# Small TensorE products and turned blocks widened to the whole 128x128 array

## The chip, the cores and the metric

The kernel runs on one core of a Trainium2 chip. The metric is the device time of one execution in microseconds (us), median over the runs shown. One further execution was taken by the hardware profiler; all rows quoted in this document that carry a time inside the kernel come from it.

## The reference

One step of a decoder layer is computed for a prompt of 512 tokens and for 8 sample sequences of 8 tokens each (64 sample tokens), 576 tokens in all, which share the weights (width 1024, fp32).

- Norm: `x * rsqrt(mean(x*x) + eps)`, ahead of and behind each of three blocks.
- Block 1 runs two mixers on one input projection. The first is a state-space scan with 16 heads and 2 groups. The second is an mLSTM with 4 heads (key width 128, value width 256): per head, `s = (q k^T) * D` with a decay matrix `D = exp(b_t - b_s + i_s - m_t)`, `num = s v + exp(..) q C`, `den = sum(s) + exp(..) q n`, `h = num / max(|den|, exp(-m_t))`, and new states `C`, `n`, `m`. The prompt starts from zero states; each sample sequence starts from states that are inputs and returns new ones.
- The mixers' normed and gated outputs go through one output projection (2048 to 1024). Block 2 is cross attention to 256 memory tokens with 4 heads of 256, block 3 a SwiGLU of hidden width 2816.
- Outputs are the 576 tokens, the memory's keys and values, and all new states.

## The kernel before

Activations are kept with features on the 128 partitions and tokens on the columns: 512 prompt columns, then 64 sample columns. A large product is made of fp32 factors split into a high and a low part, three products per 128x128 weight tile (L215, L216, L218), with weights streamed from memory.

The Python text lists the work in program order. A planner then orders the instructions of each engine along a simulated timeline: an instruction takes its turn when its inputs, its PSUM bank and its SBUF room are free, earlier ones in the text first. On the chip each engine works through its list in that order. `tc.issue_after(m)` holds instructions behind `m` on its engine. The framework puts a wait between two instructions whenever they touch an overlapping region of one tile and at least one writes it, and between the last use of a tile and the first use of another tile in the same room.

The parts that the change touches:

- **Norm rows.** `rstd_rows` (L279) turns a column of 1/rms values for each chunk of tokens into a row repeated on 128 partitions: a TensorE transpose per chunk, with the column broadcast to 128 as the stationary operand. The chunk of 64 sample tokens uses 64 rows of the array. It comes at the first norm, at the two group norms (`gn_apply`), behind the output projection, ahead of the cross attention, and once more in the tail by `root_rows1` (L2425).
- **Gates' columns.** Rows of per-token gate values, one per head, stand in `r1` (100 partitions) and in `r2` (4 partitions: the running maximum `mrw`). The transposes L617, L618, L621 and L622 turn them into `CT`, 104 columns per 128 tokens; two small products (L625, L632) with selector matrices fetch the values at chunk and sample ends.
- **State-space samples.** L788 makes one 64x64 product per group from the sample columns of `bc`.
- **mLSTM.** `qk` is one tile of 8 rows by 576 columns on 128 partitions: rows 0 to 3 are the queries of the four heads, rows 4 to 7 the keys. The prompt heads run in a loop (L957 to L1005): scores, decay, values, a chain of four 128-token states, a head norm, and at the end transposes (L1004) whose results are copied by ScalarE **over the prompt columns 0 to 511 of row h and of row 4+h of `qk`** (L1005). Behind the loop in the text come the samples: decay matrix `ds_` (L1013 to L1021), scores `ps_ss` of the four heads from columns 512 to 575 (L1024), their product (L1025), then for each half of four sequences the products with the old states (L1042 opens the sum in PSUM, L1049 adds to it), the states' update in place (`km` L1052, products L1056, VectorE L1057), the stores L1059, the product `ps_mx` of the maxima (L1066), a head norm, and a copy into columns 512 to 575 of `qk` (L1075).
- **What follows.** Gate projections (z from `z_evac` on, L1083; then og) stand later in the text. `mixs_h` and `mixs_l` (cast L202 and difference L203 in `gn_apply`) hold the first mixer's output; they lie in room that held the samples' pool `ms` and the tile `vt4_` (prompt values, and the samples' `es`). `out1` (L1181) is the output projection's first half and reads them; every later stage of block 1 reads its results.

Of the kernel before, what the change touches and what calls it, by code (L numbers as in the profile page):

```python
# [11 lines left out]
F32 = mybir.dt.float32  # L12
# [7 lines left out]
P = 128  # L20
T = 576
TP = 512
TS = 64
# [30 lines left out]
_c32 = {}  # L54
# [5 lines left out]
NC32, NLONG = _n, _c32["sgn"][0]  # L60
# [55 lines left out]
def build(nc, tc, ctx, I, O):  # L116
    V, A, G, S, TE = nc.vector, nc.scalar, nc.gpsimd, nc.sync, nc.tensor
    mm = TE.matmul
# [23 lines left out]
    def BP(name="b"):  # L142
        return pb.tile([P, 512], F32, name=name, tag="b")
# [11 lines left out]
    def C32(k):  # L155
        a, b = _c32[k]
        return c32[:, a:b] if b <= NLONG else c32e[:, a - NLONG:b - NLONG]
# [9 lines left out]
    ident, ones = C32("ident"), C32("ones")  # L167
# [65 lines left out]
    pows, ssq_mm, rops, rows = [], [], [], []  # L233
# [45 lines left out]
    def rstd_rows(rc, chunks, out, alloc=None, copy=None):  # L279

        for c0 in range(0, len(chunks), 3):
            part = chunks[c0:c0 + 3]
            b = part[0][0]
            w = part[-1][0] + part[-1][1] - b
            ps = (alloc or BP)("ps_rb")
            for j, (t0, n) in enumerate(part):
                rows.append(TE.transpose(ps[:, t0 - b:t0 - b + n], rc[:n, c0 + j:c0 + j + 1].to_broadcast([n, P]),
                                         ident[:n, :n]))
            (copy or A.copy)(out[:, b:b + w], ps[:, :w])
        return ps  # L290
# [24 lines left out]
    c32e = ml.tile([P, NC32 - NLONG], F32, name="c32e")  # L315
# [215 lines left out]
    qk = SL(1, "qk")  # L531
# [17 lines left out]
    def row(name, n=68, dt=F32, tag=None):  # L549
        return gp_.tile([n, T], dt, name=name, tag=tag or name)  # L550
# [19 lines left out]
    r1 = row("r1", 100)  # L570
# [5 lines left out]
    l2, gpr = row("l2", tag="e1"), row("gpr", tag="rmask")  # L576
    G.tensor_copy(l2[r4, :], la[r4, :])
# [5 lines left out]
    V.tensor_tensor_scan(mrw[r4, :], l2[r4, :], i2[r4, :], 0.0, op0=ALU.add, op1=ALU.max)  # L583
    G.memset(mp[r4, 0:128], 0.0)
# [29 lines left out]
    with tc.issue_after(products[140].ins), tc.high_priority(offset=1000):  # L614
        psc = MP("ps_ct")
        for c in range(4):
            TE.transpose(psc[:, c * 104:c * 104 + 100], r1[:, c * P:(c + 1) * P], ident[0:100, 0:100])  # L617
            TE.transpose(psc[:, c * 104 + 100:c * 104 + 104], r2[:, c * P:(c + 1) * P], ident[0:4, 0:4])  # L618
        A.copy(CT[:, 0:4, :], psc[:, 0:416].rearrange("p (c k) -> p c k", c=4))
        psc = MP("ps_ct2")  # L620
        TE.transpose(psc[:TS, 0:100], r1[:, TP:T], ident[0:100, 0:100])  # L621
        TE.transpose(psc[:TS, 100:104], r2[:, TP:T], ident[0:4, 0:4])  # L622
# [9 lines left out]
        mm(pse[:TS, 0:104], C32("esamp")[:TS, :], CT[:TS, 4, :], start=True, stop=True)  # L632
# [143 lines left out]
    for g in range(2):  # L776
# [11 lines left out]
        mm(pcb[:TS, :TS], bc[:, g, TP:T], bc[:, 2 + g, TP:T], start=True, stop=True)  # L788
# [233 lines left out]
    pss = BP("ps_ss")  # L1022
    for h in range(4):
        mm(pss[:TS, h * TS:(h + 1) * TS], qk[:, 4 + h, TP:T], qk[:, h, TP:T], start=True, stop=True, skip_group_check=True)  # L1024
# [7 lines left out]
    for h in range(4):  # L1032
        TE.transpose(psk[:TS, h * P:(h + 1) * P], qk[:, 4 + h, TP:T], ident)
    kws = ms.tile([TS, 4, P], F32, name="kws")
    V.tensor_tensor(kws, psk[:TS, :].rearrange("p (h k) -> p h k", h=4),
                    wendm[:TS, 4, :].unsqueeze(2).to_broadcast([TS, 4, P]), op=ALU.mult)
    for hb in range(2):
# [24 lines left out]
        m4 = ms.tile([4, 4, 32], F32, name="m4t", tag="m4t", bufs=1)  # L1062
        V.tensor_tensor(m4, C32("m4")[:4, :].rearrange("p (h t) -> p h t", h=4),
                        mrow[:, r].unsqueeze(1).to_broadcast([4, 4, 32]), op=ALU.mult)
        psx = BP("ps_mx")
        mm(psx[:, 0:1], m4.rearrange("p h t -> p (h t)"), ones[:4, :], start=True, stop=True)  # L1066
# [1355 lines left out]
    def root_rows1():  # L2422
        tail["ps"] = ps = B0("ps_rb")
        for c, (t0, n) in enumerate(HCHUNKS[1]):
            TE.transpose(ps[:, t0 - 256:t0 - 256 + n], tail["pf1"][:n, c:c + 1].to_broadcast([n, P]), ident[:n, :n])  # L2425
# [216 lines left out]
```

## Time and profile before

| | us |
|---|---|
| median of 3 runs | 1073.94 (1070.35 to 1074.08) |
| profiled execution, its own time | 1071.59 |
| its span (first to last instruction) | 1069.8 |
| TensorE busy in the span | 1060.1 |
| VectorE busy | 775.2 |
| ScalarE busy | 616.5 |
| GpSimd busy | 236.9 |

The profile names engines PE (TensorE matmul), PEld (its weight load), DVE (VectorE), ACT (ScalarE), POOL (GpSimd) and SP (SyncE, which issues most transfers); a q behind the name is the engine's sequencer. A group's row gives line, engine, operation, what it writes and reads, shapes and count, then shortest, median and longest duration in ns with the first and the last start in us. A row of the timeline gives the start in us and the duration in us; a matmul's duration covers its way through the array and overlaps the next, so the time that one takes from the engine is the distance between starts. "64*128 64x64" of a matmul means a stationary operand of 64 rows and 128 columns, and a moving operand of 64 rows and 64 columns.

### The profile page before, as it was taken

The page shows a single profiled execution, that of the slowest core. Times are in us where ns is not written, and L with a number is a line of the kernel's source. Part 1 is how long each engine was busy: PE and PEld are TensorE (multiplying, and loading weights), DVE is VectorE, ACT ScalarE, POOL GpSimd, SP SyncE. Part 2 cuts the span into 40 slices and gives each one's busy share as a digit, 9 for nine tenths or more (in the row PEclk, how much of TensorE's full clock was granted, in tenths as well). Part 3 has the DMA queues.
Part 4 walks back from the last instruction along what each step waited for, and adds up shares of the span by engine and source line. Part 5 has one row for each costly group of instructions (what it writes and reads, how often), then busy time and mean ns, then how long its engine had stood idle before and what let it go on. Part 6 is the DMA issues. An engine that isn't in the chain of part 4 may idle for free.

```text
span 1069.8 us, 20670 instructions
## 1 busy us (share of the span) xinstructions
PE 1060.1 (99%) x8060; PEld 1006.9 (94%) x8060; DVE 775.2 (72%) x1554; ACT 616.5 (58%) x1115; POOL 236.9 (22%) x308
## 2 busy tenths in 40 slices
PE   9999999999999999999999999999999999999997
PEld 8999887778999999999999989999999999999997
DVE  6798675658887898779755556776467887787556
ACT  6778533446654557666555535545566566656654
POOL 0453643313123131010244201100011111111000
PEclk9999999999999999999999999999999999999999
DMA  6676544426654349784568775743476688578532
GB/s 209 164 172 133 160 128 171 155 69 189 192 155 139 98 128 245 289 285 139 174 208 290 269 245 177 263 119 100 128 178 141 157 191 176 117 190 187 145 120 89
DMA packets 59829, 184.10 MB, mean 172 GB/s; under 512 B 6700, under 2 KB 12204, under 8 KB 59220
## 3 DMA queue, kind: packets, MB, share of 16 engines
q1 hardware_dynamic: 43316, 139.79, 39.2%
q0 software_dynamic: 15840, 42.21, 20.8%
q8 instruction: 63, 1.03, 0.4%
q10 hardware_dynamic: 576, 0.79, 0.2%
q14 instruction: 34, 0.28, 0.1%
HBM read 162.11 MB, written 20.65 MB: 171 GB/s over the span
## 4 chain that ended last, share of the span: by engine, by line
PE 96%; DVE 2%; DMA 1%; issue 0%; ACT 0%; SPq 0%; POOL 0%; DVEq 0%; POOLq 0%
PE ps_in L218 7%; PE ps_in L215 7%; PE ps_in L216 6%; PE ps_v L882 5%; PE ps_g L2111 3%; PE ps_u L2111 3%; PE ps_g L2110 3%; PE ps_u L2112 3%; PE ps_g L2112 3%; PE ps_u L2110 3%; PE ps_dn L2110 2%; PE ps_dn L2112 2%; PE ps_dn L2111 2%; PE ps_dn L215 2%; PE ps_dn L218 2%; PE ps_o L218 2%
## 5 line engine op out<-in xcount | busy, mean ns | idle before, releaser
L215 PE MATMUL ps_in<-uh,whi 128*128 128x320 f32 (+1 forms) x544 | 162.5, 299 | 0.0
L218 PE MATMUL ps_in<-uh,wlo 128*128 128x320 f32 (+1 forms) x544 | 162.1, 299 | 0.0
L216 PE MATMUL ps_in<-ul,whi 128*128 128x320 f32 (+1 forms) x544 | 161.3, 297 | 0.0
L191 ACT CAST whi<-raw 128x1024 fp32r<-128x1024 f32 (+1 forms) x98 | 99.1, 1013 | 83.6 <-PE ps_in L216 15.9
L198 DVE TENSOR_TENSOR wlo<-raw,whi 128x512 fp32r<-128x512 f32 (+2 forms) x91 | 86.7, 953 | 54.1 <-ACT whi L191 53.0
L218 PEld LDWEIGHTS ps_in<-uh,wlo 128*128 128x128 f32 x544 | 102.1, 188 | 2.3 <-issue 1.3
L215 PEld LDWEIGHTS ps_in<-uh,whi 128*128 128x128 f32 x544 | 102.2, 188 | 1.8 <-issue 0.8
L216 PEld LDWEIGHTS ps_in<-ul,whi 128*128 128x128 f32 x544 | 102.4, 188 | 0.5
L196 POOL DMA_DIRECT2D wlo<-win x31 | 27.3, 881 | 79.8 <-ACT wlo L195 72.6
L2110 PE MATMUL ps_g<-b,whi 128*128 128x288 f32 x144 | 42.4, 295 | 0.0
L2111 PE MATMUL ps_g<-b,whi 128*128 128x288 f32 x144 | 42.3, 294 | 0.0
L2111 PE MATMUL ps_u<-b,whi 128*128 128x288 f32 x144 | 42.2, 294 | 0.0
L2110 PE MATMUL ps_u<-b,whi 128*128 128x288 f32 x144 | 42.2, 294 | 0.0
L2070 DVE TENSOR_TENSOR wlo<-sw,whi 128x1024 fp32r<-128x1024 f32 (+1 forms) x26 | 29.6, 1140 | 17.1 <-ACT whi L2069 11.8
L2083 ACT CAST whi<-rawx 128x1024 fp32r<-128x1024 f32 (+1 forms) x26 | 25.6, 986 | 26.1 <-PE ps_dn L2111 13.3
L2060 ACT CAST whi<-raw 128x1024 fp32r<-128x1024 f32 (+1 forms) x26 | 25.6, 984 | 23.0 <-PE ps_g L2111 11.8
L198 POOL TENSOR_TENSOR wlo<-raw,whi 128x512 fp32r<-128x512 f32 x17 | 29.9, 1764 | 38.1 <-ACT whi L191 38.0
L215 PE MATMUL ps_xo<-qh,whi 128*128 128x288 f32 x128 | 38.2, 301 | 0.0
L216 PE MATMUL ps_xo<-ql,whi 128*128 128x288 f32 x128 | 37.8, 297 | 0.0
L216 PE MATMUL ps_o<-mixm_l,whi 128*128 128x256 f32 (+1 forms) x128 | 37.5, 293 | 0.0
L215 PE MATMUL ps_xq<-u2h,whi 128*128 128x320 f32 (+1 forms) x128 | 37.5, 295 | 0.0
L215 PE MATMUL ps_o<-mixm_h,whi 128*128 128x256 f32 (+1 forms) x128 | 37.4, 293 | 0.0
(828 smaller groups left out, 3898.4 us busy)
## 6 DMA issues: line engine op xcount, KB each, us to landing
raw<-win SPq DMA_DIRECT2D x35, 512.0 KB, 3.9
raw<-wout SPq DMA_DIRECT2D x14, 512.0 KB, 5.9
raw<-wxq SPq DMA_DIRECT2D x13, 512.0 KB, 5.3
raw<-wgate SPq DMA_DIRECT2D x13, 512.0 KB, 4.5
raw<-wup SPq DMA_DIRECT2D x13, 512.0 KB, 5.2
wlo<-win POOLq DMA_DIRECT2D x24, 256.0 KB, 5.2
kva<-vc SPq DMA_DIRECT2D x11, 512.0 KB, 6.3
raw<-wv SPq DMA_DIRECT2D x10, 512.0 KB, 3.9
```

Source lines behind the costliest of these rows:

```text
L191: casts.append(A.copy(hi[:, :n], raw[:, :n]))
L196: accs.append(G.dma_start(lo[:, a:b], src[:, a:b], accum_op=ALU.add))
L198: e.tensor_tensor(lo[:, a:b], raw[:, a:b], hi[:, a:b].bitcast(F32), op=ALU.subtract)
L215: mm(ps, wh, ah, start=i == 0, stop=False)
L216: products.append(mm(ps, wh, al, start=False, stop=False))
L218: m = mm(ps, tiles[order[c]][1], xh(order[c], t0, n), start=False, stop=c == len(tiles) - 1)
L882: mm(ps, a, b, skip_group_check=True, **kw)
L2060: s.c1 = A.copy(s.h1[:, s.all], s.r1[:, s.all])
L2070: V.tensor_tensor(s.l2[:, s.all], sw[:, s.all], s.h2[:, s.all].bitcast(F32), op=ALU.subtract)
L2110: mm(ps, wh, b[0][k], start=start and k == 0, stop=False, skip_group_check=True)
L2111: mm(ps, wh, b[1][k], start=False, stop=False, skip_group_check=True)
L2112: m = mm(ps, wl, b[0][k], start=False, stop=k == nk - 1, skip_group_check=True)
```

## The change

Operands that used part of the array are widened.

- A norm row's last chunk is turned from all 128 rows of the column, with the whole identity; 128 columns are written where 64 are used.
- `r1` has 104 partitions. GpSimd issues a transfer that copies `mrw` into partitions 100 to 103, and one transpose takes the place of each pair. `r2` stays for its other readers. `CT`'s unused partitions 64 to 127 of the sample block are zeroed, and L632 takes 128 rows and 128 columns of its selector.
- L788 takes 128 columns of `bc` instead of 64 as its stationary operand.
- The samples' scores take 128 columns of `qk` from column 512 on. A row has 576 columns, so the view runs over columns 512 to 575 of row 4+h and columns 0 to 63 of row 5+h. Row 7 has no next row; its 64 columns are copied by GpSimd to a zeroed tile `k3`.
- The maxima's factor `m4` is one zeroed tile of 128 partitions, of which four are filled, for both halves.

```diff
             for j, (t0, n) in enumerate(part):
-                rows.append(TE.transpose(ps[:, t0 - b:t0 - b + n], rc[:n, c0 + j:c0 + j + 1].to_broadcast([n, P]),
-                                         ident[:n, :n]))
+                rows.append(TE.transpose(ps[:, t0 - b:t0 - b + P], rc[:, c0 + j:c0 + j + 1].to_broadcast([P, P]), ident))
...
-    r1 = row("r1", 100)
+    r1 = row("r1", 104)
...
+    G.memset(CT[TS:P, 4, :], 0.0)
...
     V.tensor_tensor_scan(mrw[r4, :], l2[r4, :], i2[r4, :], 0.0, op0=ALU.add, op1=ALU.max)
+    G.dma_start(r1[100:104, :], mrw[r4, :])
...
         for c in range(4):
-            TE.transpose(psc[:, c * 104:c * 104 + 100], r1[:, c * P:(c + 1) * P], ident[0:100, 0:100])
-            TE.transpose(psc[:, c * 104 + 100:c * 104 + 104], r2[:, c * P:(c + 1) * P], ident[0:4, 0:4])
+            TE.transpose(psc[:, c * 104:c * 104 + 104], r1[:, c * P:(c + 1) * P], ident[0:104, 0:104])
...
-        TE.transpose(psc[:TS, 0:100], r1[:, TP:T], ident[0:100, 0:100])
-        TE.transpose(psc[:TS, 100:104], r2[:, TP:T], ident[0:4, 0:4])
+        TE.transpose(psc[:TS, 0:104], r1[:, TP:T], ident[0:104, 0:104])
...
-        mm(pse[:TS, 0:104], C32("esamp")[:TS, :], CT[:TS, 4, :], start=True, stop=True)
+        e0 = _c32["esamp"][0] - NLONG
+        mm(pse[:, 0:104], c32e[:, e0:e0 + P], CT[:, 4, :], start=True, stop=True)
...
-        mm(pcb[:TS, :TS], bc[:, g, TP:T], bc[:, 2 + g, TP:T], start=True, stop=True)
+        mm(pcb[:, :TS], bc.rearrange("p g t -> p (g t)")[:, g * T + TP:g * T + TP + P], bc[:, 2 + g, TP:T], start=True, stop=True)
...
+    k3 = ms.tile([P, P], F32, name="k3s")
+    G.memset(k3[:, TS:P], 0.0)
+    G.tensor_copy(k3[:, 0:TS], qk[:, 7, TP:T])
     for h in range(4):
-        mm(pss[:TS, h * TS:(h + 1) * TS], qk[:, 4 + h, TP:T], qk[:, h, TP:T], start=True, stop=True, skip_group_check=True)
+        k0 = (4 + h) * T + TP
+        mm(pss[:, h * TS:(h + 1) * TS], k3 if h == 3 else qk.rearrange("p j t -> p (j t)")[:, k0:k0 + P], qk[:, h, TP:T],
+           start=True, stop=True, skip_group_check=True)
...
+    m4 = ms.tile([P, 4, 32], F32, name="m4t")
+    G.memset(m4, 0.0)
...
-        m4 = ms.tile([4, 4, 32], F32, name="m4t", tag="m4t", bufs=1)
-        V.tensor_tensor(m4, C32("m4")[:4, :].rearrange("p (h t) -> p h t", h=4),
+        V.tensor_tensor(m4[:4], C32("m4")[:4, :].rearrange("p (h t) -> p h t", h=4),
                         mrow[:, r].unsqueeze(1).to_broadcast([4, 4, 32]), op=ALU.mult)
         psx = BP("ps_mx")
-        mm(psx[:, 0:1], m4.rearrange("p h t -> p (h t)"), ones[:4, :], start=True, stop=True)
+        mm(psx[:, 0:1], m4.rearrange("p h t -> p (h t)"), ones, start=True, stop=True)
...
         for c, (t0, n) in enumerate(HCHUNKS[1]):
-            TE.transpose(ps[:, t0 - 256:t0 - 256 + n], tail["pf1"][:n, c:c + 1].to_broadcast([n, P]), ident[:n, :n])
+            TE.transpose(ps[:, t0 - 256:t0 - 256 + P], tail["pf1"][:, c:c + 1].to_broadcast([P, P]), ident)
```

## The prediction

> **What bounds the kernel now.** I read the page's shares and the chain of waits first, then TensorE's timeline around each product that the change widens, then the groups of the mLSTM's samples, heads and successors.
>
> The page, busy shares and the chain that ended last:
>
> ```profile
> PE 1060.1 (99%) x8060; PEld 1006.9 (94%) x8060; DVE 775.2 (72%) x1554; ACT 616.5 (58%) x1115; POOL 236.9 (22%) x308
> PE 96%; DVE 2%; DMA 1%; issue 0%; ACT 0%; SPq 0%; POOL 0%; DVEq 0%; POOLq 0%
> ```
>
> TensorE sets the end nearly everywhere: whatever it is spared is gained, and whatever leaves it without work is lost, because nothing later has slack to give back.
>
> **What narrow products cost.** TensorE's timeline at a lone narrow norm row (L287), a pair of maxima products (L1066) and the gates' blocks:
>
> ```profile
> 524.30 0.28 PE L218 MATMUL ps_xq<-u2h,wlo 128*128 128x256 f32 x1
> 524.41 0.28 PE L215 MATMUL ps_xq<-u2h,whi 128*128 128x256 f32 x1
> 524.62 0.27 PE L287 MATMUL ps_rb<-c,p_r 64*128 64x64 f32 x1
> 524.82 0.38 PE L216 MATMUL ps_xq<-u2l,whi 128*128 128x256 f32 x1
> 525.04 0.28 PE L218 MATMUL ps_xq<-u2h,wlo 128*128 128x256 f32 x1
> ...
> 302.62 0.31 PE L218 MATMUL ps_in<-uh,wlo 128*128 128x320 f32 x1
> 302.86 0.38 PE L1066 MATMUL ps_mx<-c,m4t 4*128 4x1 f32 x2
> 303.17 0.41 PE L215 MATMUL ps_in<-uh,whi 128*128 128x320 f32 x1
> 303.42 0.31 PE L216 MATMUL ps_in<-ul,whi 128*128 128x320 f32 x1
> ...
> 81.25 0.25 PE L617 MATMUL ps_ct<-c,r 100*128 100x100 f32 x1
> 81.43 0.22 PE L618 MATMUL ps_ct<-c,r 4*128 4x4 f32 x1
> ...
> 83.06 0.42 PE L218 MATMUL ps_in<-uh,wlo 128*128 128x320 f32 x1
> 83.32 0.31 PE L215 MATMUL ps_in<-uh,whi 128*128 128x320 f32 x1
> ```
>
> The reader is to look at distances between starts. 128x256 products follow one another at 0.11 us (524.30 to 524.41). Around the narrow row they are 0.21, 0.20 and 0.22: the engine loses time going in, in the product, and coming out.
>
> Prices of the same work on the whole array, from the chain (a transpose block) and two groups (one-column sums; the scores):
>
> ```profile
> 284.03 0.87 PE ps_ht L1004 x8
> ...
> L241 PE MATMUL ps_ss<-c,ssqx x10: 250/250/271, 25.9 to 26.9; 128*128 128x1 f32 x10
> ...
> L1024 PE MATMUL ps_ss<-qk x8: 221/222/270, 224.3 to 224.7; 128*64 128x64 f32 x8
> ```
>
> A full transpose takes 0.87/8 = 0.11 us; a full product with one column takes (26.9 - 25.9)/9 = 0.11 per pass, so its 128-column weight load sets it; a score pass with 64 columns takes (224.7 - 224.3)/7 = 0.06.
>
> **The sum of the savings.**
> - Norm rows: 0.21 + 0.20 + 0.22 - 2 x 0.11 = 0.41 now, 0.11 after, 0.30 saved. Six of them (first norm, two group norms, behind the output projection, ahead of the attention, tail): 1.8 us.
> - Maxima: from 302.62 to 303.42 is 0.80, of which two 128x320 products at 0.15 are 0.30; 0.50 now, two passes of 0.11 after, 0.28 saved, twice: 0.6.
> - Gates: 81.25 to 83.32 less one product of 0.15 is 1.92 for ten transposes. After it four full ones (0.44) and one that still writes 64 partitions (0.11 + 0.30 for going in and out): 0.85. Saved 1.1. The selector product L632: two passes and two switches, like the maxima, 0.3. L788, two groups, likewise 0.3 each at the most, 0.5 together.
> - Scores: entry and exit saved (0.3 or less), but eight passes go from 0.06 to 0.11, which costs 0.4. Between -0.2 and +0.2; I take 0, the two rows being close.
>
> Together 4.3 us; 3 if the exits turn out to be other waits, 5 at the most.
>
> **What is added, at no cost while it is covered.** The zeroing and the copy for `k3`, `m4` and `CT` go to GpSimd, 22% busy, long ahead of use. The transfer of `mrw` waits on GpSimd's queue for the scan; ScalarE's copy of `sx` is the last writer of `r1` today:
>
> ```profile
> 73.74 1.35 DVE L583 TENSOR_TENSOR_SCAN mrw<-l,i 4x576 f32<-4x576 f32 x1
> ...
> 75.21 0.86 POOL L196 DMA_DIRECT2D wlo<-win  x1 [5.21 <-DVE mrw L583]
> ...
> 80.27 0.67 ACT L595 COPY r<-sx 4x576 f32<-4x576 f32 x1
> ...
> wlo<-win POOLq DMA_DIRECT2D x24, 256.0 KB, 5.2
> ```
>
> The scan ends at 75.1; issue 0.9 and landing 5.2 (a far larger transfer, so an upper bound) give 81.2 at the latest, against 80.9 for `sx` and 81.25 for the first transpose. A weight transfer (75.21) is queued behind it and moves 0.9 back. While either is late, TensorE has input projection products to run, so I cost both at 0; without that cover, 0.3 and 0.9 us.
>
> **The new wait.** The view for head h reads columns 0 to 63 of row 5+h. ScalarE writes these at the end of prompt head h+1 (L1005), and that copy stands earlier in the text, so TensorE must now wait for it: score 0 for head 1, score 1 for head 2, score 2 for head 3, the last. L1025 needs all four. Groups of the heads and of the samples, then VectorE's and ScalarE's steps:
>
> ```profile
> L971 PE MATMUL ps_s<-qk x32: 270/275/276, 250.6 to 351.7; 128*128 128x128 f32 x32
> L1005 ACT COPY qk<-ps_ht x8: 571/589/595, 285.6 to 385.6; 128x512 f32<-128x512 f32 x8
> ...
> 317.52 1.07 ACT L1005 COPY qk<-ps_ht 128x512 f32<-128x512 f32 x2 [0.36 <-PE ps_ht L1004]
> 347.30 1.07 ACT L1005 COPY qk<-ps_ht 128x512 f32<-128x512 f32 x2 [1.24 <-PE ps_ht L1004]
> ...
> L1025 DVE TENSOR_TENSOR ds__3161<-ds__3161,ps_ss x1: 402/402/402, 259.6 to 259.6; 64x256 f32<-64x256 f32 x1
> L1061 DVE COPY nums<-ps_nh x2: 419/423/427, 267.2 to 315.1; 128x257 f32<-128x257 f32 x2
> L1052 ACT ACTIVATE km<-sta,c x8: 708/724/726, 261.9 to 338.9; 96x512 fp32r<-96x512 f32 x8
> L1057 DVE SCALAR_TENSOR_TENSOR c<-c,vt,ps_cu x32: 473/477/486, 265.8 to 345.4; 128x258 f32<-128x258 f32 x32
> ```
>
> Today the scores run at 224.3 and the samples run inside the heads' time: L1025 at 259.6, the last state update at 345.4, while the last head's copy starts at 385.6. After the change everything from L1025 on starts behind that copy. Queued behind it by data are the sums L1042 and L1049, the in-place updates L1057 (the old state must be read first), the stores, and then whoever wants the samples' room:
>
> ```profile
> 365.40 0.37 ACT L1075 COPY qk<-ps_hts 128x256 f32<-128x256 f32 x1
> ...
> L202 ACT CAST mixs_h<-xs x8: 667/674/680, 365.7 to 369.7; 128x576 fp32r<-128x576 f32 x8
> L203 DVE TENSOR_TENSOR mixs_l<-xs,mixs_h x8: 745/752/806, 367.0 to 373.8; 128x576 fp32r<-128x576 f32 x8
> L215 PE MATMUL ps_o<-mixs_h,whi x32: 276/304/367, 385.0 to 397.1; 128*128 128x256 f32 x16, 128*128 128x320 f32 x16
> ```
>
> The casts start 0.3 us after the samples' last copy; they are their successor in the same room. TensorE reaches their product at 385.0, so today 19.3 us lie between.
>
> Working out when that product can start:
> - Heads: the copies of heads 1 and 2 are 347.30 - 317.52 = 29.8 us apart. Four such steps from 250.6, plus the pair of copies 1.1, give 371. Without the samples' share of VectorE they may be shorter (32 updates x 0.48 = 15 us in about 100, so 25 each: 352); as now, 386.
> - Samples behind it: from L1025 to `nums` 267.2 - 259.6 = 7.6 among other work, I take 6; per sequence `km` 0.72, four updates 4 x 0.48 and 0.7 for handing over, 3.3, times eight 26.7; 5 between the halves, whose split operands (`stacks`) have one buffer; 2 at the end. Together 40. Bounds: 33 without any handing over; 60, half way to today's 106 (259.6 to 365.4) among all the other work.
> - Casts and differences 0.67 + 0.75, and then the product runs at the pace of eight differences, 6.0, instead of its own 8 x 3 x 0.11 = 2.7: 4.7.
>
> 371 + 40 + 4.7 = 415.7, against 385.0: **30.7 us late**. Gate projections stand ahead of this in TensorE's order and need no more time than today, so nothing is left to fill the gap; all later work moves along. Bounds: 352 + 33 + 4.7 gives 5 us, 386 + 60 + 4.7 gives 66 us. I take the middle one, since its head step is measured and its updates are too.
>
> [...] The last slice of the profile, where TensorE runs dry, has a lower granted clock, and everything around it has a full one:
>
> ```profile
> 1050.00:1060.00 10.00, 10.00 (x90) 10.00 (x89) 7.80 (x14) 5.67 (x13) 0.00 (x0) 1.00 0.34 122
> 1060.00:1070.00 10.00, 2.98 (x25) 2.50 (x23) 4.31 (x12) 1.40 (x4) 0.00 (x0) 0.83 0.28 105
> ```
>
> (Columns: busy PE, PEld, DVE, ACT, POOL; then the granted clock 1.00 and 0.83.) [...]
>
> Net 30.7 - 4.3 = +26.4. The profiled execution took 1071.6 (span 1069.8, 1.8 around it), so 1098.0; the runs' median is 1073.9, 2.3 above that execution, and I leave the forecast at **1098 us**.
>
> **Rivals.**
> - *The stall is hidden; only the savings count.* The samples' late start would have to fit ahead of 385.0, so the heads would have to end by about 340. For it: VectorE loses 15 us of competing work there. Against it: each head's chain of four states is serial, and no head took under 29.8. 1071.6 - 4.3 = 1067.3. Chance 0.10. This is the case on the other side, and it also holds if the planner sees no overlap of the regions.
> - *The samples stay as slow behind the heads as within them.* Output gating and the sums for the next stage still want VectorE, and the state transfers (a store, then a load into the same buffer) would pace each half. The decisive point is whether a sequence takes over 5 us instead of 3.3: eight times 2 and a slower start and end give 60 instead of 40, 1118; with the heads at 386, 1133. Chance 0.13.
> - *The gates' transfer lands late.* If a small transfer took over 6 us and the input products ran out, the mixers would start up to 3 us later: 1101 with the stall, 1070 without. Chance of the second 0.03.
> - *Widening saves nothing.* If the switches are paid elsewhere, since other narrow products stay: 1102 with the stall, 1072 without it; the second has 0.02.
>
> **Chances and range.** The main case has 0.72, with 1079 to 1120 as its own range. No change means within 0.5%, about 5.4 us, of the median 1073.9. 1067.3 is 6.6 below it but only 4.3 below the profiled execution, so the hidden case is split: 0.05 faster, 0.05 same. Same gets 0.05 more from the small cases and 0.03 from the main case's low end: 0.13; slower 0.82. The range leaves out the hidden case, part of the slow one and the extremes: 1072 to 1121.
>
> **What would show it.** The scores L1024 start after the last L1005 copy instead of at 224, in four steps behind heads 1 to 3. TensorE has idle time between the last gate projection and `ps_o<-mixs_h`, ended by the casts or by VectorE, 20 to 45 us. The head step falls below 31 us. Narrow rows at 0.11 between starts, with no wide gap around them, would confirm the savings; the gates' block at 0.9 instead of 1.9. The prediction is wrong if the scores still start near 224, if TensorE stays above 98% busy, or if the heads end near 340.

## The result, and the profile after

The changed kernel takes 1111.1 us (median of 4 runs, 1109.5 to 1113.0) against 1072.6 for the kernel before on the same chip (4 runs, one more than in the table ahead of the prediction): ratio 1.0368, 95% interval 1.0353 to 1.0383. That is 38.6 us more, and the span of the profiled execution grew by the same amount, from 1069.8 to 1108.4. The forecast was 1098: slower was right, and the time lies within the range, but the loss is half as large again as forecast. One execution among all those below (1150.6 us at a mean granted clock of 0.85, in the run with more cover) stands apart and has no part in the ratios.

In the changed file the lines behind the edits stand four to seven lower: the scores are L1028, their product with the decay L1030, the sums L1049 and L1056, `km` L1059, the state products L1063 and updates L1064, the maxima L1072, the samples' turned blocks and their copy L1080 and L1081. L1005 is still the heads' last copy.

The page of the changed kernel: busy shares, TensorE's row and its granted clock in 40 slices, the chain that ended last.

```profile
PE 1073.5 (97%) x8055; PEld 1013.5 (91%) x8055; DVE 782.6 (71%) x1554; ACT 618.7 (56%) x1115; POOL 239.8 (22%) x313
PE   9999999999999858999999999999999999999997
PEclk9999999999999958999999999999999999999999
PE 84%; DVE 8%; issue 3%; ACT 3%; POOL 1%; DMA 0%; SPq 0%; DVEq 0%; ACTq 0%; POOLq 0%
```

TensorE still issues the same work, but slices 14 to 16 (about 360 to 443 us) show holes, and the clock falls to half in slice 15 (388 to 416 us). VectorE's and ScalarE's share of the chain rises from 2% and 0% to 8% and 3%. So there is one place to look at. The windows around it (columns: busy PE, PEld, DVE, ACT, POOL; then granted clock, DMA share, GB/s):

```profile
380.00:400.00 20.00, 10.07 (x47) 5.21 (x47) 11.64 (x32) 6.79 (x11) 0.88 (x2) 0.59 0.58 182
400.00:420.00 20.00, 12.39 (x60) 6.04 (x60) 9.29 (x28) 3.42 (x8) 1.15 (x2) 0.59 0.45 167
```

The groups that answer to those of the prediction (shortest, median and longest ns, first and last start):

```profile
L1005 ACT COPY qk<-ps_ht x8: 581/590/606, 284.3 to 376.4; 128x512 f32<-128x512 f32 x8
...
L1028 PE MATMUL ps_ss<-qk x6: 222/275/323, 318.9 to 377.2; 128*128 128x64 f32 x6
L1030 DVE TENSOR_TENSOR ds__3158<-ds__3158,ps_ss x1: 403/403/403, 377.9 to 377.9; 64x256 f32<-64x256 f32 x1
L1064 DVE SCALAR_TENSOR_TENSOR c<-c,vt,ps_cu x32: 470/482/485, 380.1 to 415.3; 128x258 f32<-128x258 f32 x32
L202 ACT CAST mixs_h<-xs x8: 667/668/672, 420.2 to 424.2; 128x576 fp32r<-128x576 f32 x8
L215 PE MATMUL ps_o<-mixs_h,whi x32: 276/304/581, 420.9 to 434.8; 128*128 128x256 f32 x16, 128*128 128x320 f32 x16
```

The scores, at 224 us before, now run from 318.9 to 377.4. The whole chain of the samples starts at 377.9 instead of 259.6, the casts at 420.2 instead of 365.7, and the output projection at 420.9 instead of 385.0. TensorE's timeline shows who ends each wait (in brackets: idle time before, and the releaser):

```profile
377.03 0.43 PE L1028 MATMUL ps_ss<-qk 128*128 128x64 f32 x2 [1.05 <-ACT qk L1005]
...
378.39 0.64 PE L1049 MATMUL ps_nh<-vts,ds__3158 32*32 32x257 f32 x8 [0.70 <-DVE ds__3158 L1030]
...
399.29 0.69 PE L1080 MATMUL ps_hts<-c,hns 128*128 128x128 f32 x2 [5.38 <-DVE hns L1077]
399.91 1.08 PE L1049 MATMUL ps_nh<-vts,ds__3158 32*32 32x257 f32 x8
...
407.13 0.80 PE L1063 MATMUL ps_cu<-stb,km 96*128 96x258 f32 x2 [0.87 <-ACT km L1059]
...
410.13 0.80 PE L1063 MATMUL ps_cu<-stb,km 96*128 96x258 f32 x2 [0.87 <-ACT km L1059]
...
419.08 0.69 PE L1080 MATMUL ps_hts<-c,hns 128*128 128x128 f32 x2 [3.03 <-DVE hns L1077]
...
420.92 0.85 PE L215 MATMUL ps_o<-mixs_h,whi 128*128 128x256 f32 x2 [1.15 <-ACT mixs_h L202]
```

The last wait for the heads is the first row, as the prediction had it; then comes the samples' own serial work, and the last row is the cast. The 5.38 in the middle was not in the prediction in that size: in TensorE's list the second half's sums stand behind the turned blocks of the first half's head norm, and they started behind them (399.91 against 399.29).

### The profile page after: what moved, and what is told of

It is laid out like the page before. It is cut to its first block, busy times and chain, and to the rows that moved or that the text cites. A ratio compares the mean times of both kernels' runs of the same rounds, so it can differ in the third digit from the quotient of the medians.

```text
span 1108.4 us, 20669 instructions
## 1 busy us (share of the span) xinstructions
PE 1073.5 (97%) x8055; PEld 1013.5 (91%) x8055; DVE 782.6 (71%) x1554; ACT 618.7 (56%) x1115; POOL 239.8 (22%) x313
## 4 chain that ended last, share of the span: by engine, by line
PE 84%; DVE 8%; issue 3%; ACT 3%; POOL 1%; DMA 0%; SPq 0%; DVEq 0%; ACTq 0%; POOLq 0%
PE ps_v L882 4%; PE ps_in L215 4%; PE ps_in L218 4%; PE ps_in L216 4%; PE ps_g L2117 3%; PE ps_u L2117 3%; PE ps_g L2116 3%; PE ps_u L2118 3%; PE ps_g L2118 3%; PE ps_u L2116 3%; PE ps_dn L2116 2%; PE ps_dn L2118 2%; PE ps_dn L2117 2%; PE ps_dn L218 2%; PE ps_dn L215 2%
## 5 line engine op out<-in xcount | busy, mean ns | idle before, releaser
L215 PE MATMUL ps_in<-uh,whi 128*128 128x320 f32 (+1 forms) x544 | 161.2, 296 | 0.1
L198 DVE TENSOR_TENSOR wlo<-raw,whi 128x512 fp32r<-128x512 f32 (+2 forms) x91 | 87.6, 962 | 54.7 <-ACT whi L191 53.7
L215 PEld LDWEIGHTS ps_in<-uh,whi 128*128 128x128 f32 x544 | 102.2, 188 | 1.1 <-DVE tmp L1151 0.3
L2089 ACT CAST whi<-rawx 128x1024 fp32r<-128x1024 f32 (+1 forms) x26 | 25.6, 986 | 26.4 <-PE ps_dn L2117 13.3
L198 POOL TENSOR_TENSOR wlo<-raw,whi 128x512 fp32r<-128x512 f32 x17 | 30.0, 1765 | 38.5 <-ACT whi L191 38.4
L215 PE MATMUL ps_xo<-qh,whi 128*128 128x288 f32 x128 | 38.2, 301 | 0.0
L215 PE MATMUL ps_o<-mixm_h,whi 128*128 128x256 f32 (+1 forms) x128 | 37.5, 293 | 0.0
L215 PE MATMUL ps_xq<-u2h,whi 128*128 128x320 f32 (+1 forms) x128 | 37.4, 295 | 0.0
```

The costliest lines, as they stand in the source:

```text
L198: e.tensor_tensor(lo[:, a:b], raw[:, a:b], hi[:, a:b].bitcast(F32), op=ALU.subtract)
L215: mm(ps, wh, ah, start=i == 0, stop=False)
```

## The experiments

Every ratio below is to the kernel before, run on the same chip, with a 95% interval. Four questions were open: is it the wait alone; how does the loss grow with the lateness; does the half clock in the gap belong to the cost; and where did the forecast savings of 4.3 us go.

### Only the scores undone

```diff
-    k3 = ms.tile([P, P], F32, name="k3s")
...
     for h in range(4):
-        k0 = (4 + h) * T + TP
-        mm(pss[:, h * TS:(h + 1) * TS], k3 if h == 3 else qk.rearrange("p j t -> p (j t)")[:, k0:k0 + P], qk[:, h, TP:T],
+        mm(pss[:TS, h * TS:(h + 1) * TS], qk[:, 4 + h, TP:T], qk[:, h, TP:T],
```

> The changed kernel with the four sample scores put back to 64x64, each reading only its own head's 64 sample columns; everything else of the change stays. Theory (the whole loss comes from the wide view that reads the first 64 columns of the next row of qk, so scores wait for the heads): the samples go back inside the heads, the gap on TensorE near 377 to 421 us goes, and what is left are the savings of the other edits, forecast 4.3 us (3 to 5): about 1068 us, ratio to before 0.996. Rival A (the loss sits in another edit: the transfer of mrw, the norm rows, the gates' block): still above 1100. Rival B (the other edits save nothing that reaches the end): 1072 to 1073, ratio 1.000.

Measured: 1073.7 us, ratio 1.0023 (1.0012 to 1.0033). The scores run at 218.7 to 227.4 again and the gap is gone. So the loss was the scores, but the forecast of what is left was wrong: the other edits do not save 4 us, they cost 2. Neither theory nor rival B had that.

### The same width without the overlap

```diff
+    k4 = ms.tile([P, 4, TS], F32, name="k4s", tag="hns", bufs=1)
+    G.tensor_copy(k4, qk[:, 4:8, TP:T])
...
-        mm(..., k3 if h == 3 else qk.rearrange("p j t -> p (j t)")[:, k0:k0 + P], ...
+        mm(..., k3 if h == 3 else k4.rearrange("p h t -> p (h t)")[:, h * TS:h * TS + P], ...
```

> The changed kernel with scores still 128 columns wide, but from a copy that holds only sample keys: the four heads' 64 sample columns side by side (heads 0 to 2 read their own and the next head's sample columns, which no head writes in this copy), and the zero-padded tile for head 3 as in the change. Width, shape and number of products stay as changed; only the overlap with columns 0 to 63 of the next row is gone. Theory (the overlap costs, the width doesn't): within 1 us of the run with narrow scores, about 1068. Rival (the wide products themselves, or their place behind a GpSimd copy, make the delay): above 1100, as changed.

Measured: 1074.5 us, ratio 1.0030 (1.0018 to 1.0043); the interval overlaps that of the narrow scores. 128 columns neither cost nor save anything that can be measured; what costs is that the 128 columns were read where the heads write.

### The scores alone, and the moment alone

The kernel before with nothing but the wide scores:

> The kernel before with only the scores widened exactly as in the change (with its padded tile for head 3). Theory: it alone carries the loss, without the savings of the other edits: after's 1111.1 + 4.3 = about 1115 us (1111 to 1119), TensorE idle 35 to 45 us behind the heads. Rival (the loss needs another edit): 1072 to 1080.

And the kernel before with its 64x64 scores, only issued late:

```diff
     for h in range(4):
-        mm(pss[:TS, h * TS:(h + 1) * TS], qk[:, 4 + h, TP:T], qk[:, h, TP:T], ...
+        with tc.issue_after(ht.ins):
+            mm(pss[:TS, h * TS:(h + 1) * TS], qk[:, 4 + h, TP:T], qk[:, h, TP:T], ...
```

> The kernel before with the 64x64 scores as they are, but issued on TensorE only behind the last head's turned blocks. Nothing is widened; only the moment is that of the change. Theory (it is the moment alone): 1111 to 1117 us, with the same gap behind the heads, perhaps 1 us less as there is no wait for ScalarE's last copy. Rival (the wide reads cost in some other way, by width or by traffic): near 1074.

Measured: 1110.3 us, ratio 1.0365 (1.0351 to 1.0379), and 1110.7 us, ratio 1.0373 (1.0358 to 1.0387). The wide scores alone give the whole loss, and so do narrow ones at the same moment. The group rows of the late narrow scores, and of the output projection behind them:

```profile
L1025 PE MATMUL ps_ss<-qk x8: 222/222/270, 374.6 to 375.0; 128*64 128x64 f32 x8
...
L215 PE MATMUL ps_o<-mixs_h,whi x32: 276/306/580, 420.0 to 434.4; 128*128 128x256 f32 x16, 128*128 128x320 f32 x16
```

The product starts at 420.0, against 420.9 in the changed kernel. The first run is 5 us under the 1115 of its theory and just under its range, the second just under its own range: both theories took away savings of the other edits that, by the first experiment, are not there. With or without the other edits the ratio is the same.

### How late is too late

Heads not named in the edit read copies of sample keys (`k4`) as above; head 0 alone, or heads 0 and 1, read `qk` 128 columns wide.

```diff
+        mm(..., k3 if h == 3 else k4.rearrange("p h t -> p (h t)")[:, h * TS:h * TS + P] if h >= 1 else
+           qk.rearrange("p j t -> p (j t)")[:, k0:k0 + P], ...          # second run: h >= 2
```

> The changed kernel where only the score of head 0 reads qk 128 columns wide, so it waits for head 1's last copy alone (near 316 us); heads 1 to 3 read copies that hold only sample keys. Theory (the later the scores, the more of the samples' work stands behind the heads, and each part of it costs its length there): before, the samples took 105 us between 260 and 364 us inside the heads and 43 us behind them. From 316 to the heads' end near 378, 60% of it is done inside and 40% is left, 0.4 x 43 = 17 us behind; the first out1 product at about 396, against 387 with narrow scores: about 1073.7 + 9 = 1083 us (1078 to 1090). Rival (only a wait that outlasts the heads costs; anything earlier is hidden): 1073 to 1076. Rival (whatever starts behind head 0 is paced by the last transfer or by the order, not by the moment): above 1100.

> The same with the scores of heads 0 and 1 wide in qk, so that the scores wait for head 2's last copy (near 351 us). Theory: from 351 to 377 a quarter of the samples is done inside the heads, three quarters stand behind them, 0.75 x 43 = 32 us; about 1073.7 + 23 = 1097 us (1090 to 1104). Rival (only a wait that outlasts the heads costs): 1073 to 1078.

Measured: 1091.2 us, ratio 1.0173 (1.0155 to 1.0192), and 1104.0 us, ratio 1.0300 (1.0284 to 1.0316). The last scores and the first output product, of the first run and then of the second:

```profile
L1030 PE MATMUL ps_ss<-qk,k3s x2: 275/275/275, 321.2 to 321.3; 128*128 128x64 f32 x2
L215 PE MATMUL ps_o<-mixs_h,whi x32: 276/304/582, 402.3 to 416.4; 128*128 128x256 f32 x16, 128*128 128x320 f32 x16
```

```profile
L1030 PE MATMUL ps_ss<-qk,k3s x2: 275/275/275, 356.0 to 356.1; 128*128 128x64 f32 x2
L215 PE MATMUL ps_o<-mixs_h,whi x32: 276/304/582, 414.3 to 428.5; 128*128 128x256 f32 x16, 128*128 128x320 f32 x16
```

So a wait that ends well inside the heads costs as well, and the rival "only a wait that outlasts the heads" falls. Against narrow scores (ratio 1.0023, scores at 227) the loss in us of 1072 is 16 with scores at 321, 30 at 356 and 37 at 377: 0.39 us for each us of lateness between the first two, 0.34 between the last two. Drawn back to nothing, that line starts at about 280, so the first 53 us of lateness would be free. At 0.39 these are 21 us, near the 19.3 that lay between casts and output projection before; no run between 227 and 321 tests this. The slope is near 43/105 = 0.41, the samples' length behind the heads over their length inside. Both runs lie above the forecast (8 and 7 us). In the first, the estimate of what stands behind the heads was right (402.3 is 16 us behind the last head copy at 386.0, forecast 17), but I had let the heads end at 378 as in the changed kernel; with half the samples inside them they end at 386. The rest is the slower pace of the output projection, 3.7 us here too (402.3 to its second half at 447.3, against 385.0 to 426.3 before), which I had left out.

### The clock in the gap

```diff
     cu = mm(ps[:, 0:258], km[:, h * P:(h + 1) * P], vst[:, h * 258:(h + 1) * 258], start=True, stop=True)
+    with tc.issue_after(cu.ins):
+        for _ in range(3):
+            mm(fill[:, 0:256], uh[:, 0, 0:P], uh[:, 0, 0:256], start=True, stop=True, skip_group_check=True)
...
+    with tc.issue_after(mx.ins):                    # behind the product of the maxima
+        for _ in range(24):
+            mm(fill[:, 0:256], uh[:, 0, 0:P], uh[:, 0, 0:256], start=True, stop=True, skip_group_check=True)
```

> The changed kernel with products that nothing reads put into TensorE's waits behind the heads: three full 128x128 fp32r products of 256 columns behind each of the 32 state products, 24 behind each product of the maxima. Theory (the clock that the gap leaves, 0.59, lengthens the samples' chain): the granted clock from 380 to 420 us goes above 0.8, the gap shortens by 3 to 7 us, 1104 to 1108 us. Rival (the chain runs on VectorE and ScalarE, TensorE's clock is not on it): within 1 us of 1111, or a few us above where the added products stand in the way.

Measured: 1109.4 us, ratio 1.0336 (1.0309 to 1.0363); the interval overlaps that of the changed kernel. The same windows as above, and the output projection:

```profile
380.00:400.00 20.00, 16.01 (x126) 12.69 (x122) 13.02 (x34) 6.79 (x11) 2.02 (x2) 0.91 0.54 177
400.00:420.00 20.00, 17.69 (x132) 13.99 (x132) 10.18 (x29) 3.22 (x7) 1.15 (x2) 0.83 0.40 147
```

The clock did what was wanted, 0.91 and 0.83 in place of 0.59, and as a whole the gap did not shorten: from the last head copy (start 377.5) to the output projection (422.6) 45.1 us, against 376.4 to 420.9, 44.5, without the added products. But its parts did not stay as they were. The first state products of two sequences in a row, each of which waits for its `km`:

```profile
409.39 0.39 PE L1064 MATMUL ps_cu<-stb,km 96*128 96x258 f32 x1 [0.34 <-ACT km L1060]
...
412.09 0.39 PE L1064 MATMUL ps_cu<-stb,km 96*128 96x258 f32 x1 [0.51 <-ACT km L1060]
```

A sequence takes 2.70 us here, with the added products in it, against 3.00 in the changed kernel (407.13 to 410.13, above). From the end of the first half's last update to the second half's first it is 8.9 us against 10.1, and from the last update's end to the end of the samples' last copy 3.8 against 4.4. So the half clock does lie on the samples' chain. What this wins is lost again: the second half's updates take 13.2 us against 11.7, with a wait of 0.61 for a state's load (405.21) in them, and the casts wait another 0.86 for a VectorE product of the output gate. How much of that the added products themselves cause is not shown; what the faster clock alone is worth stays open. The ratios don't settle it either: 1.0336 and 1.0368 have intervals that just overlap, 3 us lies between them, and the profiled execution (1112.8) is 3 us above the other three (1109.2 to 1109.6). Neither the theory nor the rival is decided.

### Where the savings went: the edits apart

Two edits leave the order of TensorE's products exactly as it was (all 8060 of the trace, by what they read and write): the norm rows and the maxima.

```diff
-                rows.append(TE.transpose(ps[:, t0 - b:t0 - b + n], rc[:n, ...].to_broadcast([n, P]), ident[:n, :n]))
+                rows.append(TE.transpose(ps[:, t0 - b:t0 - b + P], rc[:, ...].to_broadcast([P, P]), ident))
...
-        mm(psx[:, 0:1], m4.rearrange("p h t -> p (h t)"), ones[:4, :], start=True, stop=True)
+        mm(psx[:, 0:1], m4.rearrange("p h t -> p (h t)"), ones, start=True, stop=True)
```

> The kernel before with only the norms' rows turned from whole 128x128 blocks and the samples' maxima over 128 rows. With these two edits TensorE's products stand in the same order as before, only their shapes differ. Theory (the narrow shapes cost what the trace of before showed; what the run with narrow scores lost came from a changed order of the products): 2.4 us saved (1.8 for rows, 0.6 for maxima), about 1069.2 us, ratio 0.9978. Rival (the drain around a narrow product is paid in another place, so nothing is saved): 1071 to 1072, ratio 1.000.

Measured: 1070.8 us, ratio 0.9984 (0.9966 to 1.0001). The runs alone don't settle it; the trace does. TensorE's timeline around the row that the prediction had shown, and around the first pair of maxima:

```profile
522.04 0.28 PE L215 MATMUL ps_xq<-u2h,whi 128*128 128x256 f32 x1
522.15 0.27 PE L287 MATMUL ps_rb<-c,p_r 128*128 128x128 f32 x1
522.18 0.36 PE L216 MATMUL ps_xq<-u2l,whi 128*128 128x256 f32 x1
522.38 0.28 PE L218 MATMUL ps_xq<-u2h,wlo 128*128 128x256 f32 x1
...
301.55 0.31 PE L218 MATMUL ps_in<-uh,wlo 128*128 128x320 f32 x1
301.69 0.28 PE L1066 MATMUL ps_mx<-c,m4t 128*128 128x1 f32 x2
301.83 0.39 PE L215 MATMUL ps_in<-uh,whi 128*128 128x320 f32 x1
302.06 0.31 PE L216 MATMUL ps_in<-ul,whi 128*128 128x320 f32 x1
```

From the product ahead of the row to the second one behind it there are 0.34 us (522.04 to 522.38), where 524.41 to 525.04 had been 0.63: 0.29 saved, 0.30 forecast. The maxima: 0.51 against 0.80, 0.29 saved, 0.28 forecast. So the price of a narrow product was read rightly.

The other two edits do change the order, because the planner lays out the whole program anew along its simulated times.

```diff
+    G.dma_start(r1[100:104, :], mrw[r4, :])
...
-            TE.transpose(psc[:, c * 104:c * 104 + 100], r1[:, c * P:(c + 1) * P], ident[0:100, 0:100])
-            TE.transpose(psc[:, c * 104 + 100:c * 104 + 104], r2[:, c * P:(c + 1) * P], ident[0:4, 0:4])
+            TE.transpose(psc[:, c * 104:c * 104 + 104], r1[:, c * P:(c + 1) * P], ident[0:104, 0:104])
```

> The kernel before with only the gates' block: mrw brought into rows 100 to 103 of r1 by a transfer, and five turns of 104 rows in place of ten. TensorE's products behind it stand in another order (178 places). Theory (the run with narrow scores lost what it saved through the changed order between the gates and the heads, and this edit is one that changes it): saves about 1 us in the block and loses 1 to 4 us between the gates and the heads, 1072 to 1075 us. Rival (this edit is free of it, another carries the loss): 1070.5 us, ratio 0.999.

```diff
-        mm(pcb[:TS, :TS], bc[:, g, TP:T], bc[:, 2 + g, TP:T], start=True, stop=True)
+        mm(pcb[:, :TS], bc.rearrange("p g t -> p (g t)")[:, g * T + TP:g * T + TP + P], bc[:, 2 + g, TP:T], start=True, stop=True)
```

> The kernel before with only the samples' B and C scores (line 788) 128 columns wide. It changes the order of TensorE's products in 24 places near the samples' state updates. Theory (order): the saving of 0.5 us is lost and with it 0 to 3 us, 1071.5 to 1074.5 us. Rival (order harmless, the forecast saving holds): 1071.1 us, ratio 0.9995.

Measured: 1075.5 us, ratio 1.0020 (1.0007 to 1.0033), for the gates' block; 1073.7 us, ratio 1.0016 (1.0000 to 1.0031), for line 788. Neither saves anything, as the theory of the order said: the gates' block alone makes the kernel slower, and line 788 probably does, with an interval that begins at 1.0000. The timeline of the gates' run near 175 us, all engines, shows how (lines here are one lower than before: L820 is GpSimd's decay of the old states, L824 VectorE's update of them, L702 the prompt's decay times scores, L709 the product that needs it):

```profile
171.95 4.28 POOL L820 TENSOR_TENSOR h<-h,vt 128x1024 f32<-128x1024 f32 x2 [5.21 <-PE ps_hs L812]
172.21 2.23 DVE L702 TENSOR_TENSOR lm<-lm,cbs 128x512 f32<-128x512 f32 x1
...
174.96 1.82 DVE L702 TENSOR_TENSOR lm<-lm,cbs 128x512 f32<-128x512 f32 x1
175.09 0.50 PE L823 MATMUL ps_hu<-stb,bm 96*128 96x512 f32 x1 [0.75 <-DVE h L824]
...
176.83 1.31 PE L709 MATMUL ps_yi<-lm,xdt 128*64 128x128 f32 x16 [1.24 <-DVE lm L702]
```

Before, the second of these state products stood behind the prompt's products, four value products later; TensorE had no wait here at all. Now it stands directly ahead of them, both need VectorE, and VectorE's multiply takes 2.23 and 1.82 us beside GpSimd's, where 0.68 is usual. These two waits are 2.0 us, and a granted clock of 0.88 and 0.95 in the windows 170 to 180 and 180 to 190 loses 1.7 more: 3.7 of the 4.0 that this stage lost. The narrow-scores run, which has all edits but one, shows the same two waits, and a third thing: the clock. The waits of TensorE between 95 and 255 us in that run (us in total, times, longest), and its window:

```profile
PE ps_yi L710 <- DVE lm L703: 1.2, 1, 1.2
PE ps_hu L824 <- DVE h L825: 0.8, 1, 0.8
PE ps_h L680 <- POOL xe L678: 0.4, 1, 0.4
```

```profile
170.00:180.00 10.00, 8.00 (x44) 5.94 (x41) 7.15 (x9) 1.63 (x3) 5.00 (x4) 0.83 0.46 172
```

Before, that window has 10.00 of TensorE and a clock of 1.00. From the first product of the state-space scan to the first of the heads, TensorE needs 150.9 us before, 155.2 in the narrow-scores run: 4.2 lost, of which 2.4 are the three waits and 1.7 is what a clock of 0.83 loses in 10 us (in the changed kernel's trace, with the same two waits, the clock is 0.50 from 176 to 178, when the waits are over and TensorE is busy throughout).

### More cover

The text holds the value products back by counts: 33 of them may go ahead of the first prompt products. If waits for VectorE are the loss, eleven more value products (2.5 us) ahead of them should fill it.

```diff
-    steps_ = [(33, inner[3]), (43, outer[1]), (60, states[4]), ...
+    steps_ = [(44, inner[3]), (48, outer[1]), (60, states[4]), ...
```

With all edits but the scores:

> The changed kernel with narrow scores, and 44 of the value products in place of 33 set ahead of the prompt's products near 175 us (48 in place of 43 ahead of the next group). Theory (the other edits' savings were eaten by TensorE's two waits for VectorE there, 0.75 and 1.25 us, and by the clock that they brought to 0.83): TensorE has 2.5 us of products to do meanwhile, the waits and the lower clock go, and about 4 us come back: 1069.5 us (1068 to 1071), ratio 0.997. Rival (the products are missing as cover in the next places, and waits appear there): 1072 to 1075.

And in the kernel before, without any of the edits:

> The kernel before with nothing but the count of value products ahead of the prompt's products raised, from 33 to 44 and from 43 to 48. Theory (the raised count only fills the wait that the other edits brought; before has no wait there): nothing to win, 1071 to 1074 us, ratio 0.999 to 1.002. Rival (the raised count is a gain of its own, and the other edits have no part in the run with more cover): 1068 to 1070 us, ratio 0.997 to 0.998.

Measured: 1070.6 us, ratio 0.9983 (0.9971 to 0.9995), with the edits; 1073.5 us, ratio 1.0007 (0.9991 to 1.0022), without. The window and the remaining waits of the first of these runs:

```profile
170.00:180.00 10.00, 10.00 (x64) 7.04 (x63) 8.43 (x11) 2.07 (x4) 4.92 (x4) 1.00 0.42 158
```

```profile
PE ps_yi L710 <- DVE lm L703: 0.8, 2, 0.6
```

The two waits near 175 and the lower clock are gone, and 4 us between ratios (1.0023 to 0.9983) came back, as the theory said. The rival is not wholly wrong: two smaller waits, 0.8 together, came up later (0.6 at 240 us, 0.2 at 249). The count is no gain by itself: in the trace of the second run the same stage takes 1.3 us longer than before, with no wait and a clock of 1.00. The first run, all edits but the scores with more cover, is the one version here that is faster than both kernels by more than its interval, by 0.17%.

The stages of the profiled executions, as us gained (minus) or lost against before, each counted from the first norm row, since the time up to it differs between executions by up to 1.8 us with no edit ahead of it. Each column is one execution, and the runs of one kernel lie up to 7 us apart (1070.4 to 1077.1 for the kernel before on the chip of the first three columns), so a column says where its time went, and the ratios say what an edit is worth:

| start of | rows, maxima | gates' block | L788 | all but scores | the same, more cover | as changed |
|---|---|---|---|---|---|---|
| state-space scan (L672) | -0.1 | -0.1 | 0.1 | -0.7 | -0.4 | -0.9 |
| heads (L971) | -0.1 | 4.0 | 2.4 | 3.5 | 0.7 | 2.7 |
| output projection | -1.0 | 4.0 | 2.5 | 2.6 | -0.2 | 37.3 |
| end | -1.9 | 4.1 | 3.5 | 2.9 | -0.8 | 39.9 |

Up to the scan the gates' block by itself saves 0.1 and all edits but the scores 0.7, the selector among them; rows and maxima save 1.9 up to the end. The gates' block and line 788, each by itself, lose more than that in a stage that they don't touch. Of the 2.4 us that line 788 loses there, 1.2 are waits at a full clock; the rest lies in longer steps between products that now have other neighbours, and I did not take it further. The selector was not run by itself.

## Why the prediction was right, and where it was wrong

**The wait** was right in each part: who is waited for (L1005 of the heads behind), in steps behind heads 1, 2 and 3 (318.9 to 377.4), what is queued behind it, that the gate projections don't fill the gap, and that the casts are the last link. The late narrow scores show that nothing else is needed. Two of its signs fit less well: TensorE is idle 19.8 of the 44.5 us between the last head copy and the output projection (20 to 45 forecast), because the samples' products fill the rest at a mean clock of 0.62, and the head step did not fall below 31 us throughout.

**The terms of the wait.** The prediction summed 371 + 40 + 4.7 and came to 30.7 us late. Measured, from the rows above:

- Heads: the last copies (375.90, a pair of 1.07) end at 377.0, not 371. The heads start 1.4 later (252.0 against 250.6) and take 125.0 in place of 120.4 (135.6 before, when the samples ran among them, so they did get shorter). The step 29.8 was the shortest of the trace before; copies of the four heads in the changed kernel start 30.5, 36.0 and 25.1 us apart, 31.3 on average from the first score. One step was taken for the mean.
- Samples: from 377.0 to the end of their last copy at 420.2, 43.2 us, not 40. The start is shorter (3.1 to the first update, 6 forecast); the eight sequences take 25.7, 26.7 forecast, 3.0 each where nothing else stands between; but 10.1 lie between the halves (5 forecast) and 4.4 behind the last update (2 forecast). In both stands the head norm, a chain of small steps, nearly all VectorE's, from the maxima to `hns`, which I had not counted step by step, and which holds TensorE's list for 5.38 and 3.03 us; the rest of the 10.1 is mostly the second half's turned blocks and sums, 4.4 us from 399.29 to the first state product at 403.65 with the clock at 0.50. (The lower bound of 33 is 34 by its own terms, 40 less 8 x 0.7.)
- Casts and pace: 0.75 to the first product and 3.7 through the slower projection, 4.4, not 4.7. The size is right by luck. The product does not run at the pace of the differences: in its new order it does six products for each of the eight differences, and after the first one it waits for none. Instead, its first 3 us go at half the clock (0.50 from 420.9 to 423.9; 0.58 in the window 420 to 425):

```profile
422.09 0.41 PE L218 MATMUL ps_o<-mixs_h,wlo 128*128 128x256 f32 x1
422.30 0.41 PE L215 MATMUL ps_o<-mixs_h,whi 128*128 128x256 f32 x1
```

The 0.21 between these starts is 0.11 at the full clock, and from its first to its last L215 the product takes 13.9 us against 12.1: 1.8 lost, about 1.5 of it to the clock and 0.3 to the wait for the first difference. Of the other 1.9, behind it, 1.6 are two waits for weights (1.25 at 440.05 for ScalarE's cast L1232, 0.30 at 448.93 for VectorE), which had been ready in time before.

So the later work (`ps_o<-mixm_h`, the projection's second half, 465.9 against 426.3) is 39.6 us late, not 30.7: 1.4 + 4.6 + 3.2 - 0.3 = 8.9 more.

**The savings** are the step that failed in kind. The prices were right one by one: 0.29 for a row and for a pair of maxima. The gates' block was even better: 79.75 to 80.37 less one product of 0.15 is 0.47, against 0.85 forecast. The rows of the changed kernel:

```profile
79.75 0.52 PE L618 MATMUL ps_ct<-c,r 104*128 104x104 f32 x4
80.11 0.25 PE L621 MATMUL ps_ct<-c,r 104*64 104x104 f32 x1
80.14 0.39 PE L218 MATMUL ps_in<-uh,wlo 128*128 128x320 f32 x1
80.37 0.31 PE L215 MATMUL ps_in<-uh,whi 128*128 128x320 f32 x1
...
84.14 0.97 PE L624 MATMUL ps_en<-CT,c32e 128*128 128x416 f32 x2 [0.79 <-ACT CT L619]
```

The five turns follow one another at 0.09 us. The sign that the prediction had named for the savings, narrow rows without a gap around them, came true while the total did not fall: it confirms the prices and not the sum. For 0.79 of the gain in the block went at once into a wait for ScalarE's copy of the block, and the reordering took the rest. The sum of 4.3 stood on the silent premise that the order of all other work stays. No term and no rival held a price for an order laid out anew, and between scan and heads it was +4.2 us in the narrow-scores run and +3.6 in the changed kernel. Counted from the first norm row, the other edits together come to +1.7 in the changed kernel's trace (2.7 lost ahead of the heads, 1.0 gained behind the start of the projection's second half) in place of -4.3. The runs, 1.0368 with them and 1.0365 without, have intervals of 1.6 us to each side: they exclude the saving of 4.3 and cannot tell +1.7 from nothing. My fourth rival, "widening saves nothing", had the right effect for the wrong reason.

26.4 forecast, 8.9 from the wait's terms, 3.3 of savings that did not come behind the heads (1.0 for 4.3): 38.6, what was measured. That it closes to a tenth proves little, since all terms are differences of the same two executions. The changed kernel's reached the first norm row 1.3 us earlier (30.1 against 31.4), with no edit ahead of it; without that the heads would be 2.7 late in place of 1.4, and the sum 39.9.

**The clock.** The prediction showed a clock of 0.83 in the last slice, and its sum has no term for the clock. The granted clock in the gap was 0.59 (windows 380 to 400 and 400 to 420), and the products behind the gap lost about 1.5 us to it. Inside the gap the samples' own products ran at 0.50 from 387 to 403 and from 408 to 424: that lies on their chain (3.00 us for a sequence; 2.70 with added products in between, where its first state product took 0.39 us in place of 0.58), and the run with a busy array does not show what it costs in all.

**The other rivals.** "Hidden" is out: the heads did not end near 340. "As slow as within" is out: a sequence takes 3.0 us, not 5. The transfer of `mrw` was not late; the turned blocks started no later than before (49.6 us behind the first norm row, 49.8 before).

## What to carry to other kernels

Before widening a read, look at who writes the extra columns and when: a value that is never used still makes an instruction wait for its writer, and here such waits cost 37 us, with the loss beginning long before the wait reached the end of what hid it. Where the order is laid out by a planner, judge a small saving only together with the order that comes out of it: compare the instruction lists, and look for new waits in stages that the edit does not touch. A copy of the wanted columns to a place of their own gave the same width without the wait (ratio 1.0030 against 1.0368).

## What the runs showed of the hardware

In the narrow-scores run two short waits of TensorE cost nearly twice their length: 0.75 and 1.25 us within 3 us, and in the 10 us window around them a granted clock of 0.83 (above), 1.7 us more. In the run of line 788, with a single wait of 1.10 us at the same place, the clock of the window is 1.00:

```profile
170.00:180.00 10.00, 8.90 (x57) 5.96 (x57) 8.07 (x14) 2.62 (x5) 5.32 (x4) 1.00 0.46 158
```

No wait of TensorE between 95 and 255 us of the narrow-scores run was longer than 1.25 us. The changed kernel has the same two waits (0.75 and 1.24 us) and the same 0.83 over 10 us; in windows of 1 us its clock is 1.00 from 170 to 175, and 0.53, 0.50, 0.50 and 0.76 from 175 to 179, which makes up the 1.7 us.

In the gates' run VectorE's multiply of two SBUF operands (median 0.68 us) took 2.23 us when it started 0.26 behind a GpSimd multiply of two operands (median 1.94; the pair took 4.28): it ended 0.55 behind the end of GpSimd's first, taken as 1.94, and the next, of 1.82, ended 0.55 behind the end of the pair. In the kernel before, the long one at this place was GpSimd's: one of its multiplies, started at 171.68, took 3.32 us, and VectorE's two beside it 0.68 each. GpSimd had started 0.25 us ahead of these two as well, but VectorE was then still in a subtraction of two SBUF operands (L198), and its multiplies followed at once:

```profile
170.79 1.22 DVE L198 TENSOR_TENSOR wlo<-raw,whi 128x1024 fp32r<-128x1024 f32 x1
171.93 1.29 DVE L703 TENSOR_TENSOR lm<-lm,cbs 128x512 f32<-128x512 f32 x2
...
L821 POOL TENSOR_TENSOR h<-h,vt x8: 1929/1937/3322, 142.9 to 191.0; 128x1024 f32<-128x1024 f32 x8
```

So which engine's multiply was the long one differs between the two orders: VectorE's by 1.55 us in the gates' run, GpSimd's by 1.38 in the kernel before. What lengthens them was not tested by a run of its own.
